# A decoder layer on one Trainium2 core: nine sevenfold pairs a pass in the down projection instead of seven, with the sums of weights for three of them made earlier and kept in DRAM

## The chip, the cores and the metric

The kernel runs on one core of one Trainium2 chip. The metric is device microseconds of an execution of the whole program; the time before is the median of three runs. The engines that matter here are TensorE (PE in the profile, its weight loads PEld), VectorE (DVE), ScalarE (ACT), GpSimd (POOL) and SyncE (SP), which only issues transfers.

## The reference, cut to what matters

One decoder layer for 256 tokens of 2048 columns, in float32: a recurrent branch and an attention branch, merged by gates, an output projection, and then the MLP, which the change is about.

```python
D_MODEL = 2048
SEQ = 256
D_FF = 4 * D_MODEL
...
        mix = sigmoid(g_rnn) * (y_rnn @ w_rnn_proj) + sigmoid(g_attn) * (y_att @ w_attn_proj)
        x = x + rmsnorm(mix @ w_out, norm_mix_post)
        h = rmsnorm(x, norm_mlp_pre)
        u = jnp.square(jax.nn.relu(h @ w_mlp_up))          # 256 x 8192
        x = x + rmsnorm(u @ w_mlp_down, norm_mlp_post)     # 8192 x 2048 weights
```

## The kernel before, in words

**Split matmuls.** Every large product is made of three matmuls: an operand is split into a high and a low part, and high x high, high x low and low x high are added up in PSUM. The weights therefore have to be split as they come in. The class `Stream` does that for all weights of the kernel in one long list of chunks of 128 x 2048 (1 MB). A chunk is loaded in two halves of 128 x 1024 (512 KB) on SP's queue into one of four rooms `wraw`; ScalarE casts the high part `whi` (L88), VectorE subtracts to get the low part `wlo` (L89), into six rooms each. The stream runs ahead of TensorE by six halves (`AHEAD`): when TensorE's code takes half j, the code splits the halves up to j + 6 and issues loads up to four raw halves beyond those. The order of the instructions on each engine is that in which the code is written, helped by a few priorities; a tile that has a fixed number of rooms makes its next writer wait for the last reader of the room that it takes.

**Order of the work.** Projections of the branches and the gates (the code from `gates` and `merge` on), the output projection, then the MLP in two halves f = 0 and 1 of the 8192 hidden columns. In each half an up projection makes 16 pairs of 128-column tiles of u, which `evacuate` squares, splits and lays out as the left-hand operand `uT[p]`; the down projection then goes over these 16 pairs twice, once for each half n of the 2048 output columns. So there are four down passes, each of 16 pairs, one chunk of weights a pair.

**Plain and sevenfold pairs.** A plain pair is 8 products of 128 x 128 by 512 (two token blocks, two column blocks of 512, two tiles of the inner dimension), three matmuls each: 24. A sevenfold pair (a pair p in `SEVEN`) computes the same with 7 products of sums (the Strassen-Winograd scheme), 21 matmuls. The sums on the left (of u) are made once in `evacuate`, which calls for 14 tiles of 128 x 128 (`seven`) instead of 8. The sums on the right are sums of the weights' four blocks B11, B12, B21, B22, which `split_sums` makes on VectorE for each such pair of each pass: one addition of 128 x 1024 (T1 and T3, L117) and two of 128 x 512 (T2, L119, written over part of the second raw half, and T4, L120). T1, T3 and T4 are the 1536 columns of `t`, whose high part `thi` ScalarE casts (L123) and whose low part `tlo` VectorE subtracts (L124). `t`, `thi` and `tlo` each take one of the twelve large rooms (`unit`, 128 x 2048 words) that the whole kernel shares.

**A pass** is the function `down`. Seven PSUM banks take the products of the sevenfold pairs; the plain pairs add to four of them (by `PLACE`). The names in the trace are `s` (two double banks: P1 and P6, Q5 and N7), `dP` (P2), `dQ` (Q3 and Q4) and `dCs`. Behind the last sevenfold pair (12) VectorE adds up the `s` banks while TensorE does the last plain pairs. The last two pairs are held back and worked through by output bank (`finish`), so that the banks are read out one after the other at the end of the pass. In the second half the result of the first is added (`early`, `acc`), and in the last pass VectorE also multiplies four quarters of `acc` by the gain `g3` (L1256), behind pairs 3, 5, 7 and 9 (`between`).

Of the kernel before, what the change touches and what calls it, by code (L numbers as in the profile page):

```python
# [18 lines left out]
F32 = mybir.dt.float32  # L19
# [19 lines left out]
SEVEN = (0, 2, 4, 6, 8, 10, 12)  # L39
# [13 lines left out]

class Stream:
# [3 lines left out]
    def __init__(self, nc, pool, chunks, room, sums):  # L58
        self.nc, self.pool, self.chunks, self.room, self.sums = nc, pool, chunks, room, sums
        self.raw, self.parts = {}, {}  # L60
        self.loaded = self.split = self.at = FIRST
        self.pin = lambda i: i
        self.high = []

    def load_to(self, n):
# [42 lines left out]
    def split_sums(self, j):  # L108


        self.load_to(j + 2)
        v = self.nc.vector
        a, b = self.raw.pop(j), self.raw.pop(j + 1)
        t = self.room(f"t{j}")[:, 0:1536]
        hi, lo = [self.room(f"t{part}{j}").bitcast(F32R)[:, 0:1536] for part in ("hi", "lo")]
        one, two, l, r = t[:, 0:1024], t[:, 1024:1536], slice(0, 512), slice(512, 1024)
        v.tensor_tensor(one.rearrange("p (a b) -> p a b", a=2), b[:, l].unsqueeze(1).to_broadcast([P, 2, 512]),  # L117
                        a.rearrange("p (a b) -> p a b", a=2), ALU.add)
        v.tensor_tensor(b[:, l], t[:, l], a[:, r], ALU.add)  # L119
        v.tensor_tensor(two, b[:, l], b[:, r], ALU.add)  # L120
        ahi, alo = self.two_parts(a, j)
        bhi, blo = self.two_parts(b, j + 1)
        self.nc.scalar.copy(hi, t)  # L123
        v.tensor_tensor(lo, t, hi.bitcast(F32), ALU.subtract)  # L124
        parts = {"B11": (ahi[:, l], alo[:, l]), "B22": (ahi[:, r], alo[:, r]), "T2": (bhi[:, l], blo[:, l]),
                 "B21": (bhi[:, r], blo[:, r])}
        for i, name in enumerate(("T1", "T3", "T4")):
            c = slice(i * 512, i * 512 + 512)
            parts[name] = hi[:, c], lo[:, c]
        self.parts[j] = parts  # L130

# [4 lines left out]
    def half(self, run_ahead=True):  # L136
        j = self.at
# [7 lines left out]
    def seven(self):  # L145

        j = self.at
        self.at += 2
        self.ahead(j)
        return self.parts.pop(j)  # L150
# [10 lines left out]
def layer(tc, x, few, kx_first, kx_rest, pos_row, gains, w_q, w_xy, w_rg, w_g, w_rp, w_ap, w_out,  # L161
# [36 lines left out]
    sums = set()  # L198
    for f in range(2):
        chunks += [w_up[32 * f + i] for i in range(32)]  # L200
        for n in range(2):
            sums.update(len(chunks) + i for i in SEVEN)
            chunks += [w_dn[(2 * f + n) * PAIRS + i] for i in range(PAIRS)]
# [106 lines left out]


# [510 lines left out]
    mixT = units("mixT")  # L822

    def merge(n, gs):

        for tb, g in enumerate(gs):
# [12 lines left out]
    ahead.append(g_rnn())  # L839
# [18 lines left out]
    away = ctx2.enter_context(tc.tile_pool(name="away", bufs=1, space=bass.MemoryType.DRAM))  # L858
# [263 lines left out]
    def down(f, n, uT, held, order, finish, early, between=lambda p: None, behind=lambda: None, closing=False):  # L1122
# [20 lines left out]
        for p in range(PAIRS - held - closing):  # L1143
            if p in SEVEN:
                parts = ws.seven()
                for name, (i, w) in LEFT.items():
# [51 lines left out]
    for f in range(2):  # L1198
        uT = {}
        rooms = [unit(f"uT{f}{i}") for i in range((PAIRS - len(SEVEN) + 1) // 2)]  # L1200
        full = []
        for p in range(PAIRS):
# [6 lines left out]
            if f == 0 and p == R2_AT:  # L1209
# [3 lines left out]
                pc = ctx2.enter_context(tc.tile_pool(name="pc", bufs=1))  # L1213
            if f == 1 or p >= R2_AT:
                for q, u in full:
                    if q in SEVEN:
                        uT[q] = pc.tile([P, 2, 7, P], F32R, tag="seven", bufs=len(SEVEN), name=f"seven{f}{q}")
                    else:
                        i = sum(k not in SEVEN for k in range(q))
                        uT[q] = rooms[i // 2][:, 2 * (i % 2) : 2 * (i % 2) + 2]  # L1220
# [28 lines left out]
        def between(p):  # L1249
# [3 lines left out]
            if p in (3, 5, 7, 9):  # L1253
                tb, q = divmod((p - 3) // 2, 2)
# [3 lines left out]
        def finish(name, b, t, at, w, fold=lambda: None):  # L1258
# [11 lines left out]
            pin(nc.scalar.activation(spare[:, p], a[:, p], AF.Square, accum_out=sq3[:, tb, k : k + 1]))  # L1270
# [22 lines left out]
        spare = flat(unit("spare", F32))  # L1293
# [83 lines left out]
```

## Time and profile before

| | |
|---|---|
| median of three runs | 1496.38 us (1496.32 to 1496.68) |
| the profiled execution | 1495.84 us, with a span of 1493.9 us |
| TensorE busy | 1484.6 us, 99% |
| weight loads | 1259.3 us, 84% |
| VectorE busy | 1097.6 us, 73% |
| ScalarE busy | 829.8 us, 56% |
| GpSimd busy | 1.7 us |
| moved by DMA | 298.28 MB, 200 GB/s over the span; read from HBM 290.69 MB, written 6.29 |
| granted TensorE clock | 0.999 |
| up projections | 818 to 978.7 and 1143.5 to 1321.2 us |
| down passes | 978.74 to 1061.02 to 1143.30, and 1321.2 to 1403.59 to 1486 us |

A row of the trace's timeline starts with the start in us and the duration in us, then the engine, the line of the kernel, the operation and its tiles (out<-in), and in brackets the idle time of the engine ahead of it with what ended it. Records of TensorE overlap, so the distance of their starts says more than their durations.

### The profile page before, as it was taken

To read this page: it belongs to the slowest core of one execution; us is meant where nothing else is said; L and a number is where in the kernel's file an instruction comes from. 1 tells how busy PE (TensorE), PEld (TensorE's weight loads), DVE (VectorE), ACT (ScalarE), POOL (GpSimd) and SP (SyncE) were. 2 spreads that over 40 slices of the span, in tenths; PEclk is the share of its full clock that TensorE was granted. 3 is DMA by queue.
4 is the path that set the end of the run, shared out by engine and by line. 5 is a ranking of instruction groups with operands and counts; after the bars stand their busy time and mean duration, and the time that the engine had idled before them with its cause. 6 is when DMAs were issued, how large, how long until landed. Compare 5 with 4: busy or idle time off the path is not lost.

```text
span 1493.9 us, 19993 instructions
## 1 busy us (share of the span) xinstructions
PE 1484.6 (99%) x7586; PEld 1259.3 (84%) x7586; DVE 1097.6 (73%) x1367; ACT 829.8 (56%) x1145; POOL 1.7 (0%) x9
## 2 busy tenths in 40 slices
PE   9999999999999999999999999999999999999997
PEld 8887778888888888888889888888888888888886
DVE  6676668759668956555658866798886666788897
ACT  8564565647467765444355655555454555555553
POOL 0000000000000000000000000000000000000000
PEclk9999999999999999999999999999999999999999
DMA  8744544555646556555764755566667555566664
GB/s 341 232 165 140 183 159 140 171 196 173 207 157 206 197 175 212 192 188 187 284 213 152 254 192 195 184 206 207 211 206 239 188 197 183 192 245 212 206 220 179
DMA packets 83903, 298.28 MB, mean 200 GB/s; under 512 B 9312, under 2 KB 9568, under 8 KB 82784
## 3 DMA queue, kind: packets, MB, share of 16 engines
q1 hardware_dynamic: 80352, 288.89, 56.6%
q10 hardware_dynamic: 3456, 8.13, 1.4%
q8 instruction: 59, 0.97, 0.3%
q14 instruction: 36, 0.29, 0.1%
HBM read 290.69 MB, written 6.29 MB: 199 GB/s over the span
## 4 chain that ended last, share of the span: by engine, by line
PE 97%; DVE 1%; ACT 1%; DMA 0%; issue 0%; DVEq 0%; ACTq 0%
PE ps L250 21%; PE ps L248 11%; PE dQ L1114 9%; PE s L1114 5%; PE dP L1114 5%; PE g L288 4%; PE g L292 4%; PE g L290 4%; PE pp L292 4%; PE pp L290 4%; PE pp L288 4%; PE dCs L1114 3%; PE q L288 2%; PE q L292 2%; PE q L290 2%; PE o L288 2%
## 5 line engine op out<-in xcount | busy, mean ns | idle before, releaser
L89 DVE TENSOR_TENSOR wlo<-wraw,whi 128x1024 fp32r<-128x1024 f32 x516 | 624.3, 1221 | 307.5 <-ACT whi L88 304.6
L88 ACT CAST whi<-wraw 128x1024 fp32r<-128x1024 f32 x516 | 536.9, 1051 | 543.0 <-PE ps L250 132.8
L250 PE MATMUL ps<-h2T,whi 128*128 128x512 f32 x960 | 223.9, 390 | 0.0
L250 PEld LDWEIGHTS ps<-h2T,whi 128*128 128x128 f32 x960 | 178.2, 188 | 35.6
L248 PEld LDWEIGHTS ps<-h2T,wlo 128*128 128x128 f32 x960 | 119.1, 192 | 2.3
L250 PE MATMUL ps<-hT,whi 128*128 128x512 f32 x512 | 120.6, 391 | 0.0
L248 PE MATMUL ps<-h2T,wlo 128*128 128x256 f32 x960 | 119.9, 283 | 0.0
L250 PEld LDWEIGHTS ps<-hT,whi 128*128 128x128 f32 x512 | 94.7, 188 | 19.5 <-issue 0.7
L1114 PE MATMUL dQ<-whi,uT 128*128 128x512 f32 (+1 forms) x288 | 105.3, 385 | 0.0
L288 PE MATMUL g<-whi,hT 128*128 128x512 f32 x256 | 101.2, 395 | 0.0
L292 PE MATMUL g<-whi,hT 128*128 128x512 f32 x256 | 99.8, 390 | 0.0
L290 PE MATMUL g<-wlo,hT 128*128 128x512 f32 x256 | 99.8, 390 | 0.0
L248 PEld LDWEIGHTS ps<-hT,wlo 128*128 128x128 f32 x512 | 63.7, 192 | 2.1 <-issue 0.8
L248 PE MATMUL ps<-hT,wlo 128*128 128x256 f32 x512 | 64.6, 283 | 0.0
L1114 PEld LDWEIGHTS dQ<-whi,uT 128*128 128x128 f32 x288 | 53.7, 188 | 10.8
L288 PEld LDWEIGHTS g<-whi,hT 128*128 128x128 f32 x256 | 48.1, 188 | 10.6 <-issue 1.0
L292 PEld LDWEIGHTS g<-whi,hT 128*128 128x128 f32 x256 | 48.1, 188 | 10.2
L290 PEld LDWEIGHTS g<-wlo,hT 128*128 128x128 f32 x256 | 48.1, 188 | 9.6
L1114 PE MATMUL dQ<-wlo,uT 128*128 128x512 f32 (+1 forms) x144 | 55.4, 385 | 0.0
L1114 PE MATMUL dCs<-whi,uT 128*128 128x512 f32 x144 | 54.1, 389 | 0.0
L1114 PE MATMUL dP<-whi,uT 128*128 128x512 f32 x144 | 53.8, 389 | 0.0
L124 DVE TENSOR_TENSOR tlo<-t,thi 128x1536 fp32r<-128x1536 f32 x28 | 49.2, 1756 | 5.8 <-ACT thi L123 5.6
(293 smaller groups left out, 2475.7 us busy)
## 6 DMA issues: line engine op xcount, KB each, us to landing
wraw<-in_w_up SPq DMA_DIRECT2D x128, 512.0 KB, 3.7
wraw<-in_w_dn SPq DMA_DIRECT2D x128, 512.0 KB, 4.1
wraw<-in_w_g SPq DMA_DIRECT2D x64, 512.0 KB, 4.4
wraw<-in_w_xy SPq DMA_DIRECT2D x64, 512.0 KB, 3.8
wraw<-in_w_q SPq DMA_DIRECT2D x32, 512.0 KB, 3.7
wraw<-in_w_ap SPq DMA_DIRECT2D x32, 512.0 KB, 3.9
wraw<-in_w_rp SPq DMA_DIRECT2D x32, 512.0 KB, 3.7
wraw<-in_w_out SPq DMA_DIRECT2D x32, 512.0 KB, 4.6
```

The costliest lines, as they stand in the source:

```text
L88: self.pin(self.nc.scalar.copy(hi, src))
L89: self.pin(self.nc.vector.tensor_tensor(lo, src, hi.bitcast(F32), ALU.subtract))
L124: v.tensor_tensor(lo, t, hi.bitcast(F32), ALU.subtract)
L248: mm(ps[:, f, 1, :], w, a[:, 0, :], start=False, stop=j == 1 and k == 7)
L250: mm(ps[:, f].rearrange("p a b -> p (a b)"), w, a.rearrange("p a b -> p (a b)"), start=kt == 0, stop=j == 3 and k == 7)
L288: mm(banks[tb][n], a[:, 0, t], hi[:, n * 512 : n * 512 + 512], start=first, stop=False)
L290: mm(banks[tb][n], a[:, 0, t], lo[:, n * 512 : n * 512 + 512], start=False, stop=False)
L292: mm(banks[tb][n], a[:, 1, t], hi[:, n * 512 : n * 512 + 512], start=False, stop=last)
L1114: mm(b, a[x], w[y], start=not begun and i == 0, stop=tail and i == 2, skip_group_check=shared)
```

## The change

`SEVEN` becomes (0, 1, 3, 4, 6, 7, 9, 10, 12): nine pairs of sixteen instead of seven. For the pairs 4, 7 and 10 of each pass (`SUMMED`, twelve chunks) the sums of weights are not made in the pass. A generator, `sums_ahead`, loads the chunk once more in an earlier stage on GpSimd's queue, adds on VectorE (`right_sums`, the same three additions) and stores the 1536 columns of sums and the 1024 columns of the changed second half to DRAM on GpSimd's queue. Six of the twelve are made while the gates are computed, three in the first up projection and three in the second; `begin` takes the generators one step further at each half or pair that TensorE's code takes. In the pass the stream then loads the changed second half from there on SP's queue, and three pieces of 128 x 512 (`second`) on GpSimd's queue.

`t`, `thi` and `tlo` now have one room each, for all pairs. The splitting of the sums is put off (`put_off`, `settle`) until the code has begun the sevenfold pair before. The products of a sevenfold pair that read the sums come first in pairs 0, 3, 6 and 9, and last in 1, 4, 7, 10 and 12. The multiplies by `g3` move to pairs 2, 5, 8 and 11. Other rooms are made later or laid elsewhere, so that the tiles find room (`mixT`, `spare`, `rooms`, `APART`, `plain`). The whole program has 7460 matmuls instead of 7484.

```diff
-SEVEN = (0, 2, 4, 6, 8, 10, 12)
+SEVEN = (0, 1, 3, 4, 6, 7, 9, 10, 12)
+SUMMED = (4, 7, 10)
+SUMS_FIRST = (0, 3, 6, 9)
+APART = (6, 7, 9, 10, 12)
...
+def right_sums(v, a, b, t):
+    l, r = slice(0, 512), slice(512, 1024)
+    one, two = t[:, 0:1024], t[:, 1024:1536]
+    v.tensor_tensor(one.rearrange("p (a b) -> p a b", a=2), b[:, l].unsqueeze(1).to_broadcast([P, 2, 512]),
+                    a.rearrange("p (a b) -> p a b", a=2), ALU.add)
+    v.tensor_tensor(b[:, l], t[:, l], a[:, r], ALU.add)
+    v.tensor_tensor(two, b[:, l], b[:, r], ALU.add)
...
     def load_to(self, n):
...
-            self.latest = self.nc.sync.dma_start(t, self.chunks[j // 2][:, c])
+            summed = j % 2 and self.summed.get(j // 2)
+            self.latest = self.nc.sync.dma_start(t, summed[1] if summed else self.chunks[j // 2][:, c])
...
     def split_sums(self, j):
...
+        summed = self.summed.get(j // 2)
+        if summed:
+            pieces = []
+            for i in range(3):
+                c = slice(i * 512, i * 512 + 512)
+                pieces.append((c, self.room("second")))
+                self.nc.gpsimd.dma_start(pieces[i][1], summed[0][:, c])
+        else:
+            t = self.sums_room("t")
+            right_sums(v, a, b, t)
+            pieces = [(slice(0, 1536), t)]
+        (ahi, alo), (bhi, blo) = self.two_parts(a, j), self.two_parts(b, j + 1)
...
-        self.nc.scalar.copy(hi, t)
-        v.tensor_tensor(lo, t, hi.bitcast(F32), ALU.subtract)
+        def split():
+            hi, lo = [self.sums_room(n).bitcast(F32R) for n in ("thi", "tlo")]
+            for c, t in pieces:
+                self.nc.scalar.copy(hi[:, c], t)
+                v.tensor_tensor(lo[:, c], t, hi[:, c].bitcast(F32), ALU.subtract)
...
+        self.put_off.append((self.last_sums, split))
+        self.last_sums = j
+        self.settle()
+
+    def settle(self):
+        while self.put_off and self.put_off[0][0] < self.now:
+            self.put_off.pop(0)[1]()
+
+    def begin(self):
+        self.now = self.at
+        self.settle()
+        if self.side and next(self.side[0], self) is self:
+            self.side.pop(0)
...
+    def sums_ahead(c, first, second, room):
+        w = flat(unit("early", F32))
+        nc.gpsimd.dma_start(w, chunks[c])
+        for _ in range(first):
+            yield
+        t = room()
+        right_sums(nc.vector, w[:, 0:1024], w[:, 1024:2048], t)
+        nc.gpsimd.dma_start(ws.summed[c][0], t)
+        nc.gpsimd.dma_start(ws.summed[c][1], w[:, 1024:2048])
+        for _ in range(second):
+            yield
...
+    ws.side += [sums_ahead(c, 5, 4, lambda: flat(unit("early_t", F32))[:, 0:1536]) for c in summed[:6]]
...
+                names = list(LEFT)
+                if p in SUMS_FIRST:
+                    names.sort(key=lambda name: LEFT[name][1] not in ("T1", "T3", "T4"))
+                else:
+                    names.sort(key=lambda name: LEFT[name][1] in ("T1", "T3", "T4"))
...
+                ws.room = u2
+                ws.sums_room = lambda tag: pc.tile([P, 1536], F32, tag=tag, name=tag)
+                ws.side += [sums_ahead(c, 7, 4, lambda: ws.sums_room("t")) for c in summed[6:9]]
...
-            if p in (3, 5, 7, 9):
-                tb, q = divmod((p - 3) // 2, 2)
+            if p in (2, 5, 8, 11):
+                tb, q = divmod(p // 3, 2)
```

The first place in the order of the program is VectorE's at the start of the fourth pass, from the third readout of the old pass (`acc<-dQ`) on. Before, L117, L119 and L120 are the sums, L89 the low parts of weights, L124 that of the sums, L1264 the readouts of the old pass and L1256 the multiply by the gain.

```order
L1264 TENSOR_TENSOR acc_11451<-dQ_11459,t 128x512
L117 TENSOR_TENSOR t_12071<-wraw_12069,wraw_11991 128x1024
L89 TENSOR_TENSOR wlo_12062<-wraw_11959,whi_12061 128x1024
L1264 TENSOR_TENSOR acc_11451<-dCs,t 128x512
L89 TENSOR_TENSOR wlo_12066<-wraw_11961,whi_12065 128x1024
L119 TENSOR_TENSOR wraw_12069<-t_12071,wraw_11991 128x512
L89 TENSOR_TENSOR wlo_12078<-wraw_11991,whi_12077 128x1024
L120 TENSOR_TENSOR t_12071<-wraw_12069 128x512
L89 TENSOR_TENSOR wlo_12082<-wraw_12069,whi_12081 128x1024
L89 TENSOR_TENSOR wlo_12126<-wraw_12087,whi_12125 128x1024
L124 TENSOR_TENSOR tlo_12073<-t_12071,thi_12072 128x1536
```

In the new program the same place reads as follows, with L61, L63 and L64 for the sums, L105 for the low parts of weights, L151 for those of the sums, L1342 for the readouts and L1334 for the multiplies.

```order
L1342 TENSOR_TENSOR acc_11645<-dQ_11653,t 128x512
L61 TENSOR_TENSOR t<-wraw_12191,wraw_12189 128x1024
L105 TENSOR_TENSOR wlo_12296<-wraw_12189,whi_12295 128x1024
L1342 TENSOR_TENSOR acc_11645<-dCs,t 128x512
L63 TENSOR_TENSOR wraw_12191<-t,wraw_12189 128x512
L1334 TENSOR_TENSOR acc_11645<-acc_11645,g_12315 128x512
L64 TENSOR_TENSOR t<-wraw_12191 128x512
L105 TENSOR_TENSOR wlo_12300<-wraw_12191,whi_12299 128x1024
L105 TENSOR_TENSOR wlo_12304<-wraw_12221,whi_12303 128x1024
L105 TENSOR_TENSOR wlo_12323<-wraw_12307,whi_12322 128x1024
L151 TENSOR_TENSOR tlo<-t,thi 128x1536
L105 TENSOR_TENSOR wlo_12359<-wraw_12309,whi_12358 128x1024
```

The sums behind that readout belonged to pair 2 and now belong to pair 1; the multiply by the gain stands among them; and their low part stands behind three low parts of weights in a row, those of pair 1's second half and of pair 2's two.

The second place is VectorE's in the middle of a pass, the first one. Before, from the low parts ahead of a sevenfold pair's sums to the low part of those sums:

```order
L117 TENSOR_TENSOR t_9280<-wraw_9233,wraw_9225 128x1024
L89 TENSOR_TENSOR wlo_9287<-wraw_9225,whi_9286 128x1024
L119 TENSOR_TENSOR wraw_9233<-t_9280,wraw_9225 128x512
L120 TENSOR_TENSOR t_9280<-wraw_9233 128x512
L89 TENSOR_TENSOR wlo_9291<-wraw_9233,whi_9290 128x1024
L89 TENSOR_TENSOR wlo_9334<-wraw_9264,whi_9333 128x1024
L89 TENSOR_TENSOR wlo_9338<-wraw_9266,whi_9337 128x1024
L124 TENSOR_TENSOR tlo_9282<-t_9280,thi_9281 128x1536
```

And now, for a pair with fetched sums (`second`), with the sums of the next pair between:

```order
L151 TENSOR_TENSOR tlo<-t,thi 128x1536
L105 TENSOR_TENSOR wlo_9051<-wraw_8991,whi_9050 128x1024
L61 TENSOR_TENSOR t<-wraw_9036,wraw_9034 128x1024
L105 TENSOR_TENSOR wlo_9069<-wraw_8993,whi_9068 128x1024
L63 TENSOR_TENSOR wraw_9036<-t,wraw_9034 128x512
L151 TENSOR_TENSOR tlo<-second,thi 128x512 x3
L64 TENSOR_TENSOR t<-wraw_9036 128x512
L105 TENSOR_TENSOR wlo_9108<-wraw_9034,whi_9107 128x1024
L105 TENSOR_TENSOR wlo_9112<-wraw_9036,whi_9111 128x1024
L105 TENSOR_TENSOR wlo_9145<-wraw_9054,whi_9144 128x1024
L105 TENSOR_TENSOR wlo_9149<-wraw_9072,whi_9148 128x1024
L151 TENSOR_TENSOR tlo<-t,thi 128x1536
```

The low parts of fetched sums come in three pieces of 512 columns, between the sums of the next pair that makes its own; the low part of those own sums then stands behind four low parts of weights.

More of the change, by code (lines that the diff above doesn't have):

```diff
@@ L63, in __init__ @@
         self.high = []
+        self.summed, self.put_off, self.last_sums, self.now = {}, [], -1, FIRST
+        self.side = []
     def load_to(self, n):
@@ L113, in split_sums @@
         a, b = self.raw.pop(j), self.raw.pop(j + 1)
[L114 to L119, printed above, removed]
@@ L136, in half @@
     def half(self, run_ahead=True):
+        self.begin()
         j = self.at
@@ L145, in seven @@
     def seven(self):
+        self.begin()
         j = self.at
@@ L197, in layer @@
     chunks += [w_out[i] for i in range(16)]
-    sums = set()
+    sums, summed = set(), []
     for f in range(2):
@@ L309, in layer @@
     order = {}
+    away = enter(tc.tile_pool(name="away", bufs=1, space=bass.MemoryType.DRAM))
+    for c in summed:
+        ws.summed[c] = [away.tile([P, n], F32, name=f"away{n}{c}") for n in (1536, 1024)]
+    def sums_ahead(c, first, second, room):
[9 more added lines that the diff above has]
+            yield
     ctx1 = ExitStack()
@@ L1199, in layer @@
         uT = {}
-        rooms = [unit(f"uT{f}{i}") for i in range((PAIRS - len(SEVEN) + 1) // 2)]
+        rooms = []
+        if f:
+            ws.side += [sums_ahead(c, 9, 6, lambda: ws.sums_room("t")) for c in summed[9:]]
         full = []
@@ L1269, in finish @@
             pin(nc.vector.tensor_tensor(a[:, p], b[:, 0:w], t[:, p], ALU.add))
-            pin(nc.scalar.activation(spare[:, p], a[:, p], AF.Square, accum_out=sq3[:, tb, k : k + 1]))
+            if not spare:
+                spare.append(flat(unit("spare", F32)))
+            pin(nc.scalar.activation(spare[0][:, p], a[:, p], AF.Square, accum_out=sq3[:, tb, k : k + 1]))
             pin(nc.vector.tensor_tensor(t[:, p], a[:, p], g3[:, q * 512 + at : q * 512 + at + w], ALU.mult))
@@ L1292, in layer @@
         last, scaled = {}, {}
-        spare = flat(unit("spare", F32))
+        spare = []
         g3 = flat(unit("g3", F32))
```

29 lines of the change are left out of this document (18 added, 11 removed).

## The prediction

> **What bounds the kernel now.** I read the page first: the span, the busy times and the chain that ended last.
>
> ```profile
> span 1493.9 us, 19993 instructions
> PE 1484.6 (99%) x7586; PEld 1259.3 (84%) x7586; DVE 1097.6 (73%) x1367; ACT 829.8 (56%) x1145; POOL 1.7 (0%) x9
> PE 97%; DVE 1%; ACT 1%; DMA 0%; issue 0%; DVEq 0%; ACTq 0%
> ```
>
> TensorE's records leave 9.3 us of the span uncovered, and the chain is TensorE's to 97%. A busy matmul record proves little, since the records overlap, so I cut out the four down passes and then looked at single starts.
>
> ```profile
> core 0: us, PE busy (x) PEld busy (x) DVE busy (x) ACT busy (x) POOL busy (x), PEclk, DMA share, GB/s
> 978.74:1061.12 82.38, 82.38 (x365) 68.24 (x364) 70.75 (x69) 42.38 (x41) 0.00 (x0) 1.00 0.59 198
> 1061.12:1143.48 82.36, 82.36 (x365) 68.23 (x364) 65.93 (x62) 41.74 (x41) 0.00 (x0) 1.00 0.65 220
> 1321.23:1403.59 82.36, 82.36 (x365) 67.95 (x363) 71.63 (x71) 44.05 (x48) 0.00 (x0) 1.00 0.63 217
> 1403.59:1486.00 82.41, 82.41 (x382) 68.97 (x380) 73.86 (x81) 41.23 (x47) 0.00 (x0) 1.00 0.62 217
> ```
>
> No pass has a gap on TensorE, the clock is full, and VectorE is next with 66 to 74 us of 82. The starts on TensorE at the head of the first pass:
>
> ```profile
> 978.74 0.39 PE L1114 MATMUL s<-whi,seven 128*128 128x512 f32 x1
> 983.50 0.39 PE L1114 MATMUL dQ<-whi,uT 128*128 128x512 f32 x1
> 988.94 0.39 PE L1114 MATMUL s<-whi,seven 128*128 128x512 f32 x1
> ```
>
> The sevenfold pair 0 takes from 978.74 to 983.50, 4.76 us for 21 matmuls; the plain pair 1 takes 5.44 us for 24. Both are 0.2267 us a matmul, whatever waits elsewhere. A pass is then 7 x 4.76 + 9 x 5.44 = 82.3 us, which is what the windows measure. So in the passes time is the number of matmuls, as long as VectorE and ScalarE keep ahead.
>
> **What the change removes.** Two plain pairs a pass become sevenfold: 2 x 3 matmuls, 1.36 us a pass, 24 matmuls and **5.44 us** in all. No other matmul changes. That is the largest gain there can be, since nothing else on TensorE's path is shortened.
>
> **What it adds on VectorE.** The durations come from the groups by form (mean ns of one):
>
> ```profile
> L89 DVE TENSOR_TENSOR wlo<-wraw,whi 128x1024 fp32r<-128x1024 f32 x516 | 624.3, 1221 | 307.5 <-ACT whi L88 304.6
> L124 DVE TENSOR_TENSOR tlo<-t,thi 128x1536 fp32r<-128x1536 f32 x28 | 49.2, 1756 | 5.8 <-ACT thi L123 5.6
> L117 DVE TENSOR_TENSOR t<-wraw,wraw 128x1024 f32<-128x1024 f32 x28 | 34.2, 1222 | 6.9 <-DMA wraw<-in_w_dn 6.4
> L120 DVE TENSOR_TENSOR t<-wraw 128x512 f32<-128x512 f32 x28 | 19.3, 690 | 0.7
> L119 DVE TENSOR_TENSOR wraw<-t,wraw 128x512 f32<-128x512 f32 x28 | 19.2, 686 | 0.3
> L1099 DVE TENSOR_TENSOR uT<-u,uT 128x512 fp32r<-128x512 f32 x18 | 12.4, 689 | 11.5 <-ACT uT L1098 11.5
> ```
>
> A sevenfold pair that makes its own sums costs VectorE 1.22 + 0.69 + 0.69 for the sums, 2 x 1.22 for the low parts of the weights and 1.76 for those of the sums: 6.8 us against 4.76 on TensorE. A plain pair costs 2.44 against 5.44. A pair whose sums come back from DRAM costs 2.44 + 3 x 0.69 = 4.5. Before, a pass held 7 x 6.8 + 9 x 2.44 = 69.6 us of this; now it holds 6 x 6.8 + 3 x 4.5 + 7 x 2.44 = 71.4, in 80.99 us instead of 82.35. The repeating group is now three pairs (own sums, fetched sums, plain): 13.7 us of VectorE in 14.96. It fits, at 92% instead of 91%.
>
> Outside the passes VectorE gets twelve sets of sums (2.6 us each) and four more sevenfold evacuations (four more instructions each, none longer than L1099's 0.69: under 2.8 us). The room for them:
>
> ```profile
> 620.00:788.00 168.00, 168.00 (x753) 139.00 (x753) 96.92 (x99) 72.60 (x81) 0.00 (x0) 1.00 0.62 216
> 818.00:978.70 160.70, 160.70 (x929) 142.45 (x928) 119.18 (x152) 93.54 (x126) 0.00 (x0) 1.00 0.61 209
> 1143.50:1321.20 177.70, 177.70 (x1025) 157.41 (x1024) 124.66 (x148) 96.80 (x120) 0.00 (x0) 1.00 0.58 197
> ```
>
> Six sets fall around the first window, with 71 us of VectorE idle: 15.6 us. Three sets and two evacuations fall into each up projection, under 13.4 us into 41 and 53 us idle. I cost them at nothing; the cover is the six split halves by which the stream runs ahead of TensorE. If it were gone, 2.6 us a set would show.
>
> **The single rooms.** The parts of the sums (thi, tlo) now have one room each. ScalarE may begin the next thi only when TensorE has done the last product with the present one, and the code puts those three products first or last in a pair so that 24 other matmuls, 5.44 us, lie between one pair's and the next's (36 before pair 12). The steps:
>
> ```profile
> 978.27 1.49 ACT L123 CAST thi<-t 128x1536 fp32r<-128x1536 f32 x1
> ...
> 985.99 0.39 PE L1114 MATMUL dCs<-whi,uT 128*128 128x512 f32 x1
> ...
> 986.42 1.06 ACT L88 CAST whi<-wraw 128x1024 fp32r<-128x1024 f32 x1 [2.04 <-PE dCs L1114]
> ```
>
> The cast of weights at 986.42 began 0.43 us after the start of the matmul it waited for, or 0.2 us after its slot. So 0.2 + 1.49 + 1.76 = 3.45 us of the 5.44; 2.0 us are left. VectorE runs in order, so an instruction in progress takes up to 1.22 of them, and two take more.
>
> **Where it does not fit.** VectorE must have two sets of own sums ready early, since pairs 0 and 1 both make theirs. In the first and third pass it does this beside the end of an up projection. At the start of the second and fourth it also reads out the old pass. The fourth start, before:
>
> ```profile
> 1401.07 0.69 DVE L1264 TENSOR_TENSOR acc<-dQ,t 128x512 f32<-128x512 f32 x1 [0.79 <-PE dQ L1114]
> 1401.99 1.23 DVE L117 TENSOR_TENSOR t<-wraw,wraw 128x1024 f32<-128x1024 f32 x1 [0.23 <-DMA wraw<-in_w_dn]
> 1403.13 1.22 DVE L89 TENSOR_TENSOR wlo<-wraw,whi 128x1024 fp32r<-128x1024 f32 x1
> 1404.27 0.68 DVE L1264 TENSOR_TENSOR acc<-dCs,t 128x512 f32<-128x512 f32 x1
> 1404.87 1.22 DVE L89 TENSOR_TENSOR wlo<-wraw,whi 128x1024 fp32r<-128x1024 f32 x1
> ...
> 1408.35 2.35 DVE L89 TENSOR_TENSOR wlo<-wraw,whi 128x1024 fp32r<-128x1024 f32 x2
> 1410.62 1.75 DVE L124 TENSOR_TENSOR tlo<-t,thi 128x1536 fp32r<-128x1536 f32 x1
> ...
> 1414.79 1.23 DVE L117 TENSOR_TENSOR t<-wraw,wraw 128x1024 f32<-128x1024 f32 x1 [1.29 <-DMA wraw<-in_w_dn]
> ...
> 1417.67 0.68 DVE L1256 TENSOR_TENSOR acc<-acc,g 128x512 f32<-128x512 f32 x1
> ```
>
> And on TensorE there:
>
> ```profile
> 1403.59 0.39 PE L1114 MATMUL s<-whi,seven 128*128 128x512 f32 x1
> ...
> 1416.73 0.39 PE L1114 MATMUL dQ<-tlo,seven 128*128 128x512 f32 x1
> ```
>
> The pass starts on TensorE at 1403.59. The sums that begin at 1401.99 were pair 2's, whose tlo, done at 1412.37, is first read at 1416.73: 4 us to spare. In the new order the sums behind that third readout are pair 1's. I keep 1401.99 (1.6 us ahead of the pass) and count forward with 1.14 for 1024 columns and 0.62 for 512, the pace of instructions back to back (1403.13 to 1404.27; 1404.27 to 1404.87 is 0.60): sums, a low part, the last readout, sum, multiply, sum, three low parts: 1.14 + 1.14 + 4 x 0.62 + 3 x 1.14 = 8.2, so pair 1's tlo starts 6.6 us into the pass and ends at 8.2. Pair 1 reads it after pair 0, 12 matmuls and one more: 4.76 + 2.72 + 0.23 = 7.7. **Late by 0.5.** Then low part, sums, multiply, sum, multiply, sum and two low parts, 3.4 + 1.14 + 2.5 = 7.1: pair 3's tlo runs from 15.3 to 17.0. Pair 3 reads it first, at 4.76 + 4.76 + 5.44 + 0.23 + 0.5 = 15.7. **Late by 1.3.** After that the order has no multiplies, and I find each tlo 1 us or more early. The second pass has the same start without multiplies, and its first two come out 1 to 2 us early. Loss in all about **1.9 us**; bounds 0 (the lead before the pass is 1 to 2 us longer than I read off) and 5 (as much lost at the second start).
>
> The first product of a pass now goes to the bank of dQ (Q4), where it went to s (P1). That bank's readout began at 1401.07 and ended 1.8 us ahead of the pass: nothing, until VectorE is 1.8 us later there.
>
> **What it adds in transfers.** Per fetched pair: 1 MB read, 1.25 MB written, 0.75 MB read again; in all 36 MB beside 298. The DMA engines are at 0.58 to 0.65, going to about 0.7.
>
> ```profile
> wraw<-in_w_dn SPq DMA_DIRECT2D x128, 512.0 KB, 4.1
> acc_away<-t ACTq DMA_DIRECT2D x8, 256.0 KB, 3.6
> g<-in_gains SPq DMA_DIRECT2D x4, 256.0 KB, 5.2
> ...
> ACT whi L88 <- DMA wraw<-in_w_out: 15.6, 11, 6.6
> ```
>
> Where other megabytes are loaded at once (w_out), the cast waited up to 6.6 us for its weights and TensorE waited for nothing, so the lead covers such bursts. In the passes the sums wait for raw halves already (1.29 us above), with four raw rooms; I allow up to 1 us there. The new DMAs stand on GpSimd's queue, where no trace here shows one. Three pieces of 256 KB are wanted per fetched pair; pair 4's cannot start before the last up pair's u is out of its room (about 7 us into the first pass) and are cast from 14.96 + 2.04 + 0.2 = 17.2 us on, 10 us later. By the row of 3.6 us, one after the other, they land in 10.8, by 5.2 in 15.6; three at once in 3.6 to 5.2. I take the overlap, cost nothing, bounds 0 to 5.6 us a fetched pair. The Trainium skill, DMA: Bandwidth & Descriptors, section Anatomy of one DMA, fits a GpSimd DMA at 2.0 us plus bytes over 436e3; an estimate from that is 2.6 us a piece, 7.8 for three in a row, and the sum would be the same as mine; no run here shows it yet.
>
> **The sum.** 1495.84 (the profiled execution, 1.9 over its span) - 5.44 + 1.9 = 1492.3. The median shown is 0.54 higher, 1496.38: **1492.9**.
>
> **Rivals.** All hidden: the stream is further ahead than I counted, 1496.4 - 5.4 = 1490.9. For it: no gap in four passes. Against it: 92% of VectorE, two pairs with own sums in a row.
>
> The handover: one room for thi and tlo makes TensorE, ScalarE and VectorE take turns, and tlo waits behind two low parts instead of one at most. There are 7 handovers of 5.44 us a pass, 28 in all. It eats the gain from 5.44 / 28 = 0.19 us each on; at 0.4 us each (two low parts, 2.44, against the 2.0 left) it is 11.2 us: 1496.4 - 5.4 + 11.2 = 1502.2, slower. For it: every tlo stands behind low parts in the new order. Against it: those are mostly ready early, as VectorE's waits for ScalarE show little beyond the casts.
>
> GpSimd's pieces come late: each microsecond past the 10 costs the twelve fetched pairs 12 us; at one, 1496.4 - 3.5 + 12 = 1504.9. For it: VectorE idles only 8.5 us of the fourth pass, so descriptors written between its instructions would crawl. Against it: the rows above. The Trainium skill, SBUF — State Buffer, section SBUF: two separate sides, says that a VectorE instruction in a mode with two ports keeps GpSimd from writing descriptors; no run here shows it.
>
> The extra traffic delays raw halves: about 1 us for each of some four sets a pass eats the gain and no more: 1495 to 1497.
>
> **How the numbers follow.** My case 0.42 (1491.5 to 1494.5), all hidden 0.17, the handover 0.25 (1493.5 to 1503), GpSimd 0.10, raw halves 0.06. A bound of 0.2%, 3.0 us, is about what a measurement of this kernel can tell from no change: 1493.4 and 1499.4. Faster: 0.30 + 0.17 + 0.03 = 0.50. Same: 0.12 + 0.10 + 0.05 + 0.05 = 0.32. Slower: 0.12 + 0.05 + 0.01 = 0.18. The range reaches from the full gain to half way into the handover's case: 1490.8 to 1498.0; its own case alone would be 1491.5 to 1494.5.
>
> **What would show it.** Right: 24 fewer matmuls, slots of 0.2267 us, passes of 81 us but for the fourth with 82.9, gaps there ahead of the products with tlo of pairs 1 and 3. Handover: gaps of some tenths in every group of three pairs, VectorE waiting for thi. GpSimd: VectorE or ScalarE waiting for second. Wrong altogether: TensorE waiting in the gates' or up projections, or slots longer than 0.2267.

## Result, and the profile after

The changed kernel takes 1506.05 us (median of six runs, 1502.91 to 1507.84), before 1496.35 (1496.13 to 1496.68). The ratio is 1.0065, 95% interval 1.0052 to 1.0078: 9.7 us slower, where 1492.9 was forecast with a range up to 1498. The runs also spread by 5 us, where those of before spread by 0.6. The profiled execution took 1507.84 us. Far slower executions (1637 to 3020 us, of the old kernel and of two new ones) are in no ratio below, but the median of the kernel without transfers, 1496.57 us, counts one of 2371.74 and is 1496.36 without it.

The page of the changed kernel, its span, busy times and chain:

```profile
span 1506.1 us, 20243 instructions
PE 1485.7 (99%) x7562; PEld 1254.8 (83%) x7562; DVE 1132.3 (75%) x1439; ACT 843.6 (56%) x1181; POOL 40.5 (3%) x81
PE 74%; DVE 9%; DMA 9%; ACT 4%; issue 3%; DVEq 0%; ACTq 0%; SPq 0%
```

The chain was TensorE's to 97%; now 22% of it is VectorE, ScalarE and DMA. Windows cut at the starts of matmuls, from the first one of a down pass to the first behind the pair of passes (the last matmul, for the second pair), of before:

```profile
978.74:1143.30 164.56, 164.56 (x728) 136.29 (x726) 136.50 (x130) 83.94 (x81) 0.00 (x0) 1.00 0.62 209
1321.11:1485.98 164.87, 164.87 (x744) 137.03 (x743) 145.61 (x151) 85.40 (x94) 0.00 (x0) 1.00 0.63 217
```

and of the changed kernel (columns as in the prediction: length, then busy time of PE, PEld, DVE, ACT, POOL, clock, DMA share, GB/s):

```profile
980.35:1152.10 171.75, 165.64 (x715) 134.74 (x714) 139.98 (x143) 91.09 (x97) 10.21 (x19) 0.99 0.74 246
1329.91:1497.57 167.66, 164.27 (x732) 134.10 (x731) 147.81 (x159) 92.32 (x108) 8.05 (x15) 1.00 0.71 240
```

With 12 of the 24 saved matmuls in each, a pair of passes should be 2.72 us shorter, 161.84 and 162.15. The first is 9.9 us longer than that, the second 5.5. The first pass starts 1.6 us later (980.35 against 978.74), the up projection between takes 177.81 us in both, and 0.6 us more lies behind the last matmul. 1.6 + 9.9 + 5.5 + 0.6 = 17.6, less the gain of 5.4: 12.2 us, the difference of the spans (1506.1 - 1493.9).

What TensorE waited for, from the waits of the changed kernel (total, times, longest; us):

```profile
PE dQ L1174 <- DVE tlo L151: 7.6, 8, 2.1
PE dQ L1174 <- ACT thi L150: 1.8, 3, 0.9
PE ptr L889 <- DVE g L907: 1.1, 1, 1.1
```

In the passes it is the parts of the sums. By the starts of the matmuls around them, these gaps cost 11.7 of the 15.4 us that the passes lost. What VectorE waited for tells why. The first row is before's, the second the change's:

```profile
DVE t L117 <- DMA wraw<-in_w_dn: 6.4, 11, 1.3
```

```profile
DVE t L61 <- DMA wraw<-in_w_dn: 21.5, 14, 4.1
```

The sums of weights wait for raw halves three times as long, up to 4.1 us. VectorE's timeline around the longest of TensorE's waits (start, duration, instruction, idle time ahead), and TensorE's:

```profile
1025.52 1.22 DVE L105 TENSOR_TENSOR wlo<-wraw,whi 128x1024 fp32r<-128x1024 f32 x1
1030.80 1.23 DVE L61 TENSOR_TENSOR t<-wraw,wraw 128x1024 f32<-128x1024 f32 x1 [4.07 <-DMA wraw<-in_w_dn]
1031.94 1.22 DVE L105 TENSOR_TENSOR wlo<-wraw,whi 128x1024 fp32r<-128x1024 f32 x1
1033.08 0.68 DVE L63 TENSOR_TENSOR wraw<-t,wraw 128x512 f32<-128x512 f32 x1
1033.68 1.89 DVE L151 TENSOR_TENSOR tlo<-second,thi 128x512 fp32r<-128x512 f32 x3
```

```profile
1033.15 0.39 PE L1174 MATMUL dQ<-thi,seven 128*128 128x512 f32 x1
1035.62 0.50 PE L1174 MATMUL dQ<-tlo,seven 128*128 128x512 f32 x1 [2.08 <-DVE tlo L151]
```

VectorE stood 4.07 us at the sums of pair 12, whose raw half had not landed, while the fetched sums of pair 10, due first, stood behind that in its queue (the second excerpt of the order in the section on the change shows just this: three pieces of tlo between the sums of the next pair). TensorE needed them at 1033.4.

The raw halves are late because four rooms hold them and their loads take longer. DMA issues from 1064 to 1080 us, the start of the second pass (count, size, median us to landing):

```profile
wraw<-in_w_dn SPq DMA_DIRECT2D x4, 512.0 KB, 7.9
second<-away POOLq DMA_DIRECT2D x4, 256.0 KB, 5.3
acc_away<-t ACTq DMA_DIRECT2D x2, 256.0 KB, 5.7
wraw<-away SPq DMA_DIRECT2D x1, 512.0 KB, 8.3
```

Loads that took 4.1 us in the median before (4.6 from 1062 to 1078 us, the start of its second pass) took 7.9 and 8.3 here, beside pieces on GpSimd's queue and stores on ScalarE's. This is a bad stretch: over the first two passes the median of these loads went from 4.2 to 4.9, and that of the fetched halves was 6.9. A room comes free only when VectorE has made the low part of the half in it, so a late half delays the issue of the next as well.

### The profile page after: what moved, and what is told of

Same layout as the page of the kernel before. It is cut to its first block, busy times and chain, and to the rows that moved or that the text cites. A ratio compares the mean times of both kernels' runs of the same rounds, so it can differ in the third digit from the quotient of the medians.

```text
span 1506.1 us, 20243 instructions
## 1 busy us (share of the span) xinstructions
PE 1485.7 (99%) x7562; PEld 1254.8 (83%) x7562; DVE 1132.3 (75%) x1439; ACT 843.6 (56%) x1181; POOL 40.5 (3%) x81
## 4 chain that ended last, share of the span: by engine, by line
PE 74%; DVE 9%; DMA 9%; ACT 4%; issue 3%; DVEq 0%; ACTq 0%; SPq 0%
PE ps L293 21%; PE ps L291 11%; DMA wraw<-in_w_dn 6%; DVE wlo L105 4%; PE pp L335 3%; PE pp L333 3%; PE pp L331 3%; PE g L331 3%; PE g L335 3%; PE g L333 3%; ACT whi L104 2%; PE q L331 2%; PE q L335 2%; PE q L333 2%; PE o L331 2%
## 5 line engine op out<-in xcount | busy, mean ns | idle before, releaser
L105 DVE TENSOR_TENSOR wlo<-wraw,whi 128x1024 fp32r<-128x1024 f32 x516 | 623.5, 1220 | 270.4 <-ACT whi L104 266.0
L1174 PE MATMUL dQ<-whi,uT 128*128 128x512 f32 (+1 forms) x192 | 71.9, 387 | 0.0
L1174 PE MATMUL s<-whi,seven 128*128 128x512 f32 x144 | 53.5, 389 | 0.0
L331 PE MATMUL q<-whi,hT 128*128 128x512 f32 x128 | 51.1, 400 | 0.0
L1174 PE MATMUL s<-thi,seven 128*128 128x512 f32 x144 | 51.0, 395 | 0.0
L331 PE MATMUL pp<-whi,yrnn 128*128 128x512 f32 x128 | 50.0, 391 | 0.0
L335 PE MATMUL q<-whi,hT 128*128 128x512 f32 x128 | 49.9, 390 | 0.0
```

The source lines that it names most:

```text
L105: self.pin(self.nc.vector.tensor_tensor(lo, src, hi.bitcast(F32), ALU.subtract))
L331: mm(banks[tb][n], a[:, 0, t], hi[:, n * 512 : n * 512 + 512], start=first, stop=False)
L335: mm(banks[tb][n], a[:, 1, t], hi[:, n * 512 : n * 512 + 512], start=False, stop=last)
L1174: mm(b, a[x], w[y], start=not begun and i == 0, stop=tail and i == 2, skip_group_check=shared)
```

## The experiments

Two theories at first. R: the extra transfers make raw halves land late, and VectorE's queue passes that on to tlo. H: the single rooms of thi and tlo and VectorE's fuller queue do it, whatever the transfers.

**Transfers left out.** First the fetched pieces alone:

```diff
-                pieces.append((c, self.room("second")))
-                self.nc.gpsimd.dma_start(pieces[i][1], summed[0][:, c])
+                pieces.append((c, self.resident()))
```

`resident` is a view of 512 columns of `uT[15]`, which lies there anyway.

> Leaves out the 36 loads of 256 KB of fetched sums (9.4 MB): the three casts and three subtractions of a fetched pair read a resident tile instead, so the values are not the sums'. Side sums, their stores and the fetched second halves stay. Theory R (the extra transfers make the raw halves land late, and VectorE's in-order queue passes that on to tlo): half or more of the 11.7 us that TensorE waits in the passes goes, 1498 to 1501 us. Theory H (the single rooms of thi and tlo and VectorE's fuller queue do it, whatever the transfers): no change, 1505 to 1507.

Measured 1500.49 us, ratio 1.0032 (1.002 to 1.0044), in R's range, though its ten executions spread from 1497.46 to 1506.3. Then the side work alone (no `ws.side`; second halves and pieces read from the weights):

> Leaves out the side sums alone (their loads, additions and stores); the pieces are fetched as before, from the weights (wrong values, the same bytes and queue), and the second halves are the weights' own. R: the 1.3 us in the gates and the waits of the second pass at 1114 to 1116 us (2.8 us), where a side chunk's load of 1 MB stands beside the raw halves, go: 1500 to 1502.5. H: only the gates' 1.3 us: 1504 to 1505.

Measured 1499.54, ratio 1.0022 (1.0013 to 1.0032), a little under R's range. Then all of it:

> Leaves out everything that the change moves: no side sums, no stores, no fetched second halves (the weights' own are loaded), no pieces (a resident tile is read instead). Matmuls, casts and subtractions of the passes, their rooms and their order rules stay as in the change. R: 1491 to 1493.5 us, nearly the full 5.4 below before. H: TensorE still waits some 10 us in the passes, only the 1.3 us in the gates come back: 1502 to 1505.

Measured 1496.57, ratio 1.0001 (0.9992 to 1.0011). So the transfers cost 9.5 us together; leaving out the pieces alone gives 5.6, the side work alone 6.5. H's 1502 is out. But R had 1491 to 1493.5: 5.7 us of loss were left. The same kernel once more, for its profile:

> The kernel without any of the added transfers and side sums once more, for a profile of its own: it measured 1496.57 us, 5.7 above the full gain. R says that what is left is the handover at the start of the fourth pass (1.4 us as in the change's trace, at 1421 and 1423 us) and other starts where raw halves are late as before; H says gaps of some tenths at most pairs that read thi and tlo.

It took 1496.62 us in its one run. Its waits of TensorE and of VectorE, and its two pairs of passes:

```profile
PE dQ L1173 <- DVE tlo L150: 2.5, 5, 0.9
PE dQ L1173 <- ACT thi L149: 0.6, 1, 0.6
```

```profile
DVE t L61 <- DMA wraw<-in_w_dn: 11.9, 11, 2.7
```

```profile
979.35:1142.06 162.71, 162.44 (x715) 133.85 (x714) 137.96 (x140) 91.00 (x97) 0.00 (x0) 1.00 0.63 215
1319.87:1486.98 167.11, 164.08 (x732) 134.19 (x731) 148.06 (x161) 92.38 (x109) 0.00 (x0) 1.00 0.62 217
```

The first two passes lose 0.9 us, the others 5.0, and half of that at the start of the fourth. The sums still wait for raw halves, 11.9 us against 6.4 before. One reason may be that the sevenfold pairs lie closer together and take two raw halves at once; no run tests that by itself.

**All sums in the pass, and eight pairs.** `SUMMED = ()` and no side work, with nine pairs and with eight:

> Nine sevenfold pairs a pass, all with sums made in the pass, nothing fetched and no side work. VectorE then has 9 x 6.8 + 7 x 2.44 = 78.3 us of work in a pass of 81, 97%. R: no late halves, but little room: 1493 to 1500. H: worse than the change, over 1507, since each pair has the longer tlo and one room t as well.

Measured 1510.4, ratio 1.0093 (1.0078 to 1.0108). Past R's range, and in H's (over 1507). Of H's two causes the rooms don't show here: TensorE's waits for tlo come to 0.9 us, and none is for thi. The longest total of its waits is for whi (4.7 us in 7 waits): ScalarE may cast a changed second half only when VectorE's sums have written it, and waited 121.7 us for that, against 75.1 before. VectorE was busy for 91 and 93% of the two pairs of passes. H's other cause, a fuller VectorE, is the likely reading; no run parts that from its order.

> Eight sevenfold pairs a pass (0, 2, 3, 5, 7, 8, 10, 12), all with their own sums, no transfers and no side work; single rooms and the splitting put off as in the change; 12 matmuls fewer than before, 2.7 us. VectorE has 8 x 6.8 + 8 x 2.44 = 73.9 us of work in 81.7, 90.5%. R: no extra transfers, so 1493.7 to 1496. H: the handover stays in 7 places a pass: 1498 or more.

Measured 1500.79, ratio 1.0036 (1.0022 to 1.0051), a miss for R as it then stood, and H's number. No transfer was added here, and yet it lost 7 us against its count of matmuls. Its sums waited only 3.7 us for raw halves, less than before's 6.4, so the sum of those waits doesn't explain it; the longest gap on TensorE, 1.3 us for tlo at the start of the second pass, does stand behind a wait of 1.95 us for a raw half. At this point the rooms of thi and tlo could still be the cause. The kernel was not run with more raw rooms, and its loss stays open.

**VectorE's order.** Own sums enforced behind the low parts split before:

```diff
+            first = right_sums(v, a, b, t).ins
+            for i in self.low:
+                self.tc.add_manual_dep(first, i.name, mybir.DependencyInfo(
+                    mybir.DependencyClass.NoSync, mybir.DependencyReason.DATA), reason="sums behind low parts")
```

`self.low` holds the low parts of the sums that were split last.

> The change with one order enforced on VectorE: a pair's own sums stand behind the low parts of the sums that were split before, so that tlo of a fetched pair no longer waits behind an addition that waits for its raw halves. R with the queue: the wait of 2.24 us at 1035.6 and the 1.4 us of slow matmuls behind it go, the others (where the pair's own sums are late) stay: 1501 to 1503.5. If VectorE's order is no part of it: 1505 to 1507.

Measured 1502.7, ratio 1.0044 (1.0029 to 1.0059): the wait at 1035.6 is gone, as expected, those for late own sums stay.

> The change with the multiplies by the gain moved from pairs 2, 5, 8, 11 to 5, 8, 11, 12. If the start of the fourth pass loses 1.4 to 2 us because a multiply stands among the sums of pair 1, up to that comes back: 1504 to 1505.5. If the place of the multiplies is nothing: 1505 to 1507.

Measured 1504.98, ratio 1.0056 (1.0041 to 1.0071), in the first reading's range, but with an interval that overlaps the change's, and where that reading put the gain there is none: the third and fourth pass take 167.7 us in its profile, as in the change's, with the same gaps at the start of the fourth. What its profiled execution is shorter by lies ahead of the first pass (1.3 us), in the first two passes (1.0) and at the end (0.5).

**Traffic alone, and one load moved.**

> The kernel before with traffic alone added: for three sevenfold pairs a pass (4, 8, 10) three loads of 128 x 512 on GpSimd's queue into rooms that nothing reads, 36 of 256 KB, from the weights. If the traffic costs by itself, as much as in the change (3 to 5.6 us): 1499 to 1502 us. If it costs only where tlo has little to spare, nothing here, since each has some 4 us: 1496 to 1497.

Measured 1500.18, ratio 1.0025 (1.0014 to 1.0036). The kernel before, too, loses 4 us to 9.4 MB on GpSimd's queue, though nothing reads them; its sums then wait 13.9 us for raw halves, up to 3.1. So it is not a matter of thin margins in the new order alone.

```diff
-        nc.gpsimd.dma_start(w, chunks[c])
+        if late:
+            with tc.issue_after(ws.latest.ins):
+                nc.sync.dma_start(w, chunks[c])
+        else:
+            nc.gpsimd.dma_start(w, chunks[c])
```

`late` is true for the three side chunks of the second up projection. In the changed kernel they did not all keep to that stage, as the section on the change has it: GpSimd issued the first one's load at 1098.02 us and its stores at 1134, and the second one's load at 1135.44, all within the second pass. TensorE's gaps at 1114.22 and 1116.15 us lie between.

> The kernel with the own sums behind the low parts of fetched ones (1502.7 us) and one thing more: the three side chunks of the second up projection are loaded on SP's queue behind the raw halves of that stage, so none of their 1 MB loads falls into the second pass. R: the waits of 2.7 us at pair 9 of the second pass, where that load stood beside the raw halves, go: 1499.5 to 1501. If that load is not the reason: 1502 to 1503.5.

Measured 1499.96, ratio 1.0027 (1.0017 to 1.0037): 2.7 us less than with the order alone, as expected. At pair 9 one gap of 0.7 us by the starts is left, of 2.7.

**The rooms.** To make space, pairs 0, 1, 3 and 4 share one left-hand room. With it, two rooms for thi and tlo, or six raw rooms, or neither:

> The change with two rooms each for thi and tlo. To make space, the left-hand tiles of pairs 0, 1, 3 and 4 share one room (three of them are then wrong in value); all transfers and all work stay. H: ScalarE no longer waits for TensorE to give thi up, and the part of the loss that is left without transfers (some 4 us) goes: 1500 to 1503. R: the sums are late, not the rooms: 1504 to 1507.

> The change with six rooms for raw halves instead of four from the first up projection on, in the space made as for the two rooms of thi and tlo (one left-hand room for pairs 0, 1, 3, 4); thi and tlo have one room each as in the change. R: loads are issued two halves earlier, so slower loads no longer hold up the sums; most of the 9.5 us that the transfers cost go: 1496 to 1499. H: 1504 to 1507.

> Control: the change with one left-hand room for pairs 0, 1, 3 and 4 (three of them wrong in value) and nothing else, as it was under the two rooms for thi and tlo and under the six raw rooms. R: 1504 to 1508 as the change, so the 12.5 us of the six raw rooms are theirs. If sharing that room itself moves the time, by so much the other two runs are to be corrected.

Measured 1511.46 (1.01; 1.0084 to 1.0116) with two rooms for thi and tlo, 1505.0 (median of three; 1.0064; 1.0049 to 1.0079) with the shared room alone, and **1493.53** (0.9982; 0.9973 to 0.9992) with six raw rooms. The two rooms missed both ranges: they gave nothing, and were slower by a wait of their own in the third pass (`s` for VectorE's `u` of the up projection, 5.1 us, once). The six raw rooms gave 11.5 us with one room each for thi and tlo, so H has fallen. That is somewhat more than the 9.5 of all transfers: the rooms also give back part of what was lost without them. The loads land no sooner (5.1 us in the median of the first two passes), they are only issued earlier. The pairs of passes take 161.84 and 163.55 us, and TensorE's waits for the sums' parts are down to 0.3:

```profile
PE dQ L1178 <- DVE tlo L155: 0.3, 1, 0.3
```

**With every value computed.** The space for a fifth raw room (4 KB a partition) is there: the rooms of pairs 6 to 12 each leave 1 KB free, and pair 15's left-hand tiles, high and low parts of 1 KB each, go into four of them.

```diff
-                        uT[q] = pc.tile([P, 2, 2, S], F32R, tag="plain", name=f"plain{f}")
+                        uT[q] = [free[-4:-2], free[-2:]]
...
+                ws.extra = [lambda name: pc.tile([P, 1024], F32, tag="wmore", name=name)]
```

> The change, complete and with the right values, with a fifth room for raw halves: pair 15's plain left-hand tiles (4 KB a partition) go into what the rooms of pairs 6 to 12 leave free (1 KB each), and the space becomes the room. Six raw rooms gave 1493.5 us (with a left-hand room shared), four 1506. R: a load issued one half earlier covers some 2.3 us of lateness, so over half comes back: 1496 to 1500. If it was the shared left-hand room that gave the time there: 1504 to 1507.

> Five raw rooms, and both other repairs: own sums behind the low parts of fetched ones on VectorE, and the side chunks of the second up projection loaded on SP's queue behind its raw halves. R: what the fifth room doesn't cover in the second pass goes: 1494 to 1497. If the two repairs add nothing once a raw room is added: as the kernel with five rooms alone.

> As the one before, with a sixth raw room from the second up projection on, where pair 4's left-hand tiles move to a large room that is free by then. R: the third and fourth pass come to what six rooms gave (163.6 us for both): 1492.5 to 1495, below before. If the first two passes decide: as with five rooms, 1494 to 1497.

Measured 1499.15 (1.0019; 1.001 to 1.0028), 1496.06 (0.9999; 0.999 to 1.0009) and 1495.42 (0.9996; 0.9987 to 1.0005), the first two in R's range. With five rooms alone TensorE has two gaps in the first two passes (1.8 us by the starts the longer one) and none in the others; with both repairs too it has none in any pass. The last missed its range and fell into the other reading's, 1494 to 1497, but not for what happens in the passes: they lasted 161.8 and 162.0 us in its profile. What it lost lay ahead of them, 4.6 us, of which 2.5 came from a slip in these three edits (a loop's bound overwritten: one half loaded where four were asked for, x's loads ahead of three raw halves at the start) and 2.0 in the gates.

> The kernel with five and six raw rooms, the sums behind the low parts and the held side loads (1495.4 us), with a slip of its edit mended: a loop's bound was overwritten, so that one raw half was loaded where four were asked for, and at the start x's loads stood ahead of three raw halves; TensorE waited 2.2 us for it at 38 us. R: that comes back and the passes stay at their matmuls (161.9 and 162.1 us): 1492.5 to 1494, below before. If raw rooms were not the cause, loads issued earlier change nothing in the passes, and the passes go back to over 164.

> The same, with the six side chunks of the gates' phase taken further apart (8 and 6 steps instead of 5 and 4), so that loads of 1 MB and stores of 1.25 MB meet less. R: of the 1.9 us that the gates lose in 570 to 607 us half or more comes back: 1491 to 1493. If the place of side loads doesn't count there: as the kernel above.

The first measured 1492.53 (0.9977; 0.9968 to 0.9986), as expected. The second, with `sums_ahead(c, 8, 6, ...)` in the gates, measured **1491.19 us** (0.9968; 0.9956 to 0.998), faster than both kernels: 1496.14 - 5.44 would be 1490.7. Its passes, and its wait for raw halves:

```profile
979.20:1141.04 161.84, 161.84 (x716) 134.01 (x714) 138.58 (x141) 91.15 (x98) 8.07 (x15) 1.00 0.71 245
1318.85:1480.87 162.02, 162.02 (x733) 134.74 (x731) 147.84 (x162) 92.00 (x111) 8.49 (x16) 1.00 0.70 242
```

```profile
DVE t L61 <- DMA wraw<-in_w_dn: 3.0, 4, 1.2
```

VectorE does the same work in the passes as in the change (138.6 and 147.8 us), every fetched piece is still loaded, and thi and tlo still have one room each. TensorE loses nothing in the passes; the first one starts 0.5 us later than before.

## Why the prediction was wrong

**The step that failed** is the one on transfers: "In the passes the sums wait for raw halves already (1.29 us above), with four raw rooms; I allow up to 1 us there", and the cost of nothing for the rest. The sum has no term for transfers at all, not even that 1 us. Without the transfers the kernel is 9.5 us faster, and the halves were up to 4.1 us late. The row used as a cover, casts in the output projection that waited up to 6.6 us while TensorE waited for nothing, was from a stage without sums. There one late half delays one low part. In a pass the sums need both halves of a pair, and VectorE keeps its order, so one late half holds up the low parts of sums that are due sooner, and the rooms, and with them the next loads.

**The raw halves as a rival** had the mechanism and a chance of 0.06, priced at "about 1 us for each of some four sets a pass", to 1497 at most. That price doesn't come out of its own numbers: 1 us for four sets in each of four passes is 16 us, not the 5.4 of the gain, and 1496.4 - 5.4 + 16 is 1507, near what was measured. The gaps in the trace are fewer and longer (waits of VectorE up to 4.1 us, of TensorE for tlo up to 2.1), so the nearness is partly luck. The range ended at 1498, half way into the handover's case, and this rival, worked out, lay beyond it.

**The count of matmuls** was right: the two passes of 161.84 us in the best kernel are 164.56 less 2.72, the full gain.

**VectorE's 92%** was right in that it fits: the same work loses nothing with five and six raw rooms. The work of 97% (all own sums) did not fit with four.

**The single rooms** were costed at nothing, rightly: two rooms gave no time back, and in the best kernel TensorE loses nothing in the passes with one, though ScalarE waits 14.7 us there, in 14 waits, for TensorE to give thi up. The handover, which had 0.25, is refuted as the cause.

**The start of the fourth pass**, 1.9 us. In the kernel without transfers TensorE's gaps there add up to 1.8 (2.4 by the starts of the matmuls), at pairs 0 and 1, not 1 and 3. The size fits by luck, the working doesn't: the multiplies are not part of it, since moving them gave nothing, and with a fifth raw room the same order loses nothing there (with six, one wait of 0.3 us at pair 3). I had counted forward from 1401.99, an instruction that had itself waited for a raw half, and took that lead as given.

**Outside the passes** nothing was allowed. TensorE waited 1.1 us in the gates, where the side chunks' loads and stores stood beside raw halves; taking them apart gave 1.3 us (1492.53 to 1491.19; the intervals of the two ratios overlap a little).

**GpSimd's pieces** were not late: no engine's list of waits names `second` as what it waited for. Landing took 5.7 us in the median, more than either row that I went by for one, yet within the 10. Descriptors written beside a busy VectorE did not crawl either: these are the pieces' lines in the view by tile: the issue's min, median and max in ns, and the landing.

```profile
L136 POOL DMA_DIRECT2D second<-away x36: 536/536/555, 954.2 to 1453.1; - x36
...
DMA to landing us min/median/max: 2.9/5.7/8.0
```

The rule that I had named beside that rival (the Trainium skill, SBUF — State Buffer, section SBUF: two separate sides, on a VectorE mode with two ports) does not show here; no run shows whether VectorE's additions and subtractions run in such a mode. The estimate of 2.6 us a piece (the Trainium skill, DMA: Bandwidth & Descriptors, section Anatomy of one DMA) is near the quickest piece, 2.9 us from the start of its issue, and less than half of the median. The same page, section SWDGE vs HWDGE vs iDMA, says that GpSimd's transfers and the other queues' feed different queues inside each DMA engine, which takes turns between them. The trace fits that, without showing the turns: at the start of the second pass raw halves took 7.9 us in the median beside the pieces, against 4.6 there before.

**What stays open.** The part of the fifth and sixth raw room, of VectorE's order and of the held side loads in the 1491.19 us is known only from the steps above, three of them with the slip. What the kernels with eight and with nine own sums lost has no run of its own, nor have the 5.7 us left without transfers, beyond that six raw rooms give back more than the transfers cost. The cause of the two rooms' 5.1 us was not pursued.

## What to carry to other kernels

A kernel whose engines are ahead by a fixed number of rooms has a lead in bytes, not in time: before adding transfers, compare the slowest landing in a busy stretch with the work that the rooms cover, and look at the longest wait of the in-order engine that needs the most rooms at once. An edit that trades arithmetic for traffic may need more input rooms before it pays; here one or two, with the order around them, turned 9.7 us lost into 5 gained. On an in-order engine keep what is due first ahead of what waits for memory; that alone gave 3.4 us here.

## What the runs showed of the hardware

One gap of 2.08 us on TensorE cost more than itself. The windows of the changed kernel, ahead of that gap's end, behind it, and behind a gap of 1.43 us (the clock is the number ahead of the last two):

```profile
1030.00:1035.00 5.00, 3.54 (x16) 2.61 (x14) 4.20 (x6) 1.70 (x3) 0.00 (x0) 1.00 0.29 96
1035.60:1038.60 3.00, 2.98 (x9) 2.39 (x10) 3.00 (x4) 1.28 (x2) 0.00 (x0) 0.64 0.08 25
1116.10:1119.00 2.90, 2.85 (x12) 2.36 (x13) 2.27 (x2) 1.17 (x3) 0.00 (x0) 1.00 0.78 277
```

Behind the longer gap the granted clock averaged 0.64, and seven matmuls followed each other at 0.43 us instead of 0.2267: 1.4 us more, in addition to the 2.2 us of the wait itself. The length of a gap doesn't decide this alone. In the control with the shared left-hand room a gap of 2.02 us was followed by full clock, and one of 1.42 us by half:

```profile
1035.84:1038.84 3.00, 3.00 (x13) 2.46 (x14) 3.00 (x4) 2.05 (x3) 0.00 (x0) 1.00 0.06 18
1114.05:1117.05 3.00, 3.00 (x7) 2.42 (x8) 2.22 (x2) 0.19 (x1) 0.00 (x0) 0.50 0.88 303
```

The Trainium skill, TensorE: Matmul & The Clock Gate, section HAM oscillation — how this bites in real kernels, gives gaps over about 3.4 us as what lowers the clock; here it was lower behind gaps of 2.08 and 1.42 us too (and behind one of 5.09 us in the kernel with two rooms for thi and tlo, at 0.50), and the measurement decides. What else it hangs on, these runs don't show.
